# A hybrid attention and state-space layer on one core: k, its row factors and y loaded two tiles ahead, the last filler weights in front of the row factors, a head's loads tied one step earlier

## The chip, the cores and the metric

The kernel runs on 1 core of one Trainium2 chip. The metric is device time in microseconds (us) of one execution. The core's engines are TensorE (PE: matmuls, with weight loads shown apart as PEld), VectorE (DVE), ScalarE (ACT), GpSimd (POOL) and SyncE (SP). SP computes nothing here: nearly every transfer between the core's memory (SBUF) and HBM is issued by it, one after the other in a written order, and an issue that waits holds up every issue behind it. The other engines also work through their instructions in order.

## The reference

One layer over 1024 tokens of 2048 channels, batch 1, everything float32, cut to what the change touches:

```python
h = rms_norm(x, ln_gain)
q, k, v, z_att, u, z_ssm, g_att, g_ssm = split(h @ w_in)      # 2048 x 10240
q, k = rms_norm(q, q_gain), rms_norm(k, k_gain)               # rows of 64
s = q @ k.T / 8                       # 8 heads, two maps each, causal
w = softmax(s[0]) - lam * softmax(s[1])
attn = rms_norm(w @ v, subln_gain) * (1 - lam_init)
y_att = attn * silu(z_att)
y = gelu(s5_scan(u))                  # diagonal state-space branch
y_ssm = y * sigmoid(y @ w_glu + b_glu) * silu(z_ssm)
merged = sigmoid(g_att) * (y_att @ w_proj_att) + sigmoid(g_ssm) * (y_ssm @ w_proj_ssm)
out = x + merged @ w_out
```

## The kernel before

Every operand of a large matmul is split into a high and a low part (`split`: ACT copies the value to a rounded type, DVE subtracts to get the rest), and a product is three matmuls: high by high, high by low, low by high. All tiles are 128 partitions by 512 columns of float32, 256 KB each. Results that are needed later go to HBM (`d_k`, `d_ks`, `d_yg`, `d_zs`, `d_o` and so on) and come back.

The stages in order of time:

1. **Input projection.** 40 column pairs of `w_in`, in two halves of the contraction. A pair is seven products of 12 matmuls, 84 matmuls (a scheme with fewer block products than the plain one). In the second pass (`whole`) each pair's four result tiles go through an evacuation by kind: q (4 pairs), k (4), v (4), `za` (4), `zs` (4), `ga` (8), `gs` (8). Per pair DVE has 16 instructions besides: seven `w_lo`, four `value`, one `acc`, four for the result tiles. `evac_k` stores raw k to `d_k` and collects its squares. `evac_gate` for `zs` also multiplies by y, loaded from `d_yg`.
2. **k's normalisation, between the pairs of `ga` and `gs`.** `norms_k` takes 16 tiles of k: load the tile `ks` from `d_k`, load its row factors `rb` from `d_rk` (two transfers, each a row repeated over 64 partitions), multiply on DVE (L1028), split (ACT writes `sh_`, DVE writes `sl_`), store both parts. `ks` and `rb` have one buffer each, `sh_` two and `sl_` one. Tile n+1's `ks` load therefore waits for tile n's last reader, the subtraction that writes `sl_`. The y tiles of `zs` use the same single buffer as `ks`; the small tile `ny` of `qk_norms` uses that of `rb`.
3. **The sigmoid-gated linear unit** (`pg`, L1162), which writes `d_ys`.
4. **Attention, 8 heads of 8 steps** in an order of PE written out by hand. Between its matmuls stand those of a filler, the projection `w_ps` (`ps_tile`, L288), whose weights come through `branch_weights`: 64 blocks, one loaded ahead. Head h's 14 loads (q, k high, k low, v high, v low: `qs`, `kh`, `kl`, `vh`, `vl`) are tied to the exponentials of head h-1 (`marks`), two to each.
5. **The tail.** Row factors of the attention output (`fr`, `fs`) go to HBM (`d_f`) and come back repeated over 128 partitions (`pf`). `pa_inputs` loads the output (`pr`), multiplies (L1375) and splits it. Three filler tiles, kept back (`TAIL`), run on PE meanwhile: six weight blocks. Then come the projection `w_pa` (L271) and the product with `w_out` (L1409), for each half of the tokens.

Outside the hand-ordered part of PE, a scheduler decides each engine's order from the written order, the buffers and its own estimate of durations; the hardware then follows that order strictly.

Of the kernel before, what the change touches and what calls it, by code (L numbers as in the profile page):

```python
# [10 lines left out]
F32 = mybir.dt.float32  # L11
# [8 lines left out]
P = 128  # L20
# [3 lines left out]
KT = DM // P  # L24
NT = S // P
# [9 lines left out]
TAIL = 3  # L35
# [32 lines left out]
def hybrid_block(ctx: ExitStack, tc: tile.TileContext, x_t, x_n, w_t, w_v, w_glu, w_pa, w_ps,  # L68
                 w_out, small, lams, ssm_bc, out):
    nc = tc.nc  # L70
    V, A, Q, T, D = nc.vector, nc.scalar, nc.gpsimd, nc.tensor, nc.sync

    def after(ins, other):

        tc.add_manual_dep(ins.ins, other.ins.name,
                          mybir.DependencyInfo(mybir.DependencyClass.Sync, mybir.DependencyReason.DATA),
                          reason="order of loads")
# [11 lines left out]
    def split(hi, lo, src, eng=None):  # L89
        A.activation(hi, src, AF.Copy)  # L90
        (eng or V).tensor_tensor(lo, src, hi.bitcast(F32), ALU.subtract)  # L91

    def load_w(src, n, eng=None, pool=None):

        pool, bufs = (wps[0], 2) if pool is None else (pool, 4)
        raw = pool.tile([P, n, WT // n], F32, name="w_raw", tag="w_raw", bufs=bufs)
        D.dma_start(raw, src)
        hi = pool.tile([P, n, WT // n], F32R, name="w_hi", tag="w_hi")
        lo = pool.tile([P, n, WT // n], F32R, name="w_lo", tag="w_lo")
        split(hi, lo, raw, eng)  # L100
        return hi, lo
# [123 lines left out]
    d_yg = dram.tile([8, P, S], F32, name="d_yg")  # L225
    d_ys = [dram.tile([8, P, S], F32, name=f"d_ys{i}") for i in range(2)]
    d_ps = dram.tile([KT, P, S], F32, name="d_ps")
    d_o = dram.tile([H, P, S], F32, name="d_o")
# [67 lines left out]
    def branch_weights():  # L296

        def blocks():
            for n in range(2 * KT):
                for b in range(2):  # L300
                    yield load_w(w_ps[n % KT, :, 4 * b:4 * b + 4], 4, Q if n < 2 * KT - TAIL else V)
        it = blocks()
        queue = [next(it)]

        def take():
            queue.append(next(it, None))
            return queue.pop(0)
        return take

    def finished(src, t):  # L310

# [14 lines left out]
    with ExitStack() as pa_ctx:  # L326
# [315 lines left out]
        rows = [normed(k) for k in range(8, 16)]  # L642
# [290 lines left out]
        for i, (_, n) in enumerate(order):  # L933
            part(n, a, 1)
            while units < min(NPAIR, (i + 1) * NPAIR / PACE):
                ssm_step(units)
                units += 1
                if units == NPAIR:
# [3 lines left out]
                    rows = [row(xp) for _ in range(8)]  # L942
# [9 lines left out]
        ev_ctx = ExitStack()  # L952
        stg = ev_ctx.enter_context(tc.tile_pool(name="stg", bufs=2, side="right"))
        more.append(stg)
        qp = ev_ctx.enter_context(tc.tile_pool(name="qp", bufs=5, side="right"))


        rq = const.tile([P, 16, NT], F32, name="rq")
# [4 lines left out]
        def qk_norms():  # L963

            for t in range(2):
                v = stg.tile([32, 512], F32, name="nv", tag="sq")
                y = stg.tile([32, 512], F32, name="ny", tag="rb", bufs=1)
                V.tensor_scalar(v, nps[t][0:32], 1.0 / 64, EPS, ALU.mult, ALU.add)
                newton_rsqrt(stg, y, v, "nr")
                D.dma_start(d_rk[:, t * 512:(t + 1) * 512], y[16:32])  # L970
                yield
                tp = sps.tile([P, 4, 32], F32, name="rqp", tag="tr", bufs=2)
                for j in range(4):
                    T.transpose(tp[:, j], y[:, j * P:(j + 1) * P], ident[0:32, 0:32])
                V.tensor_copy(rq[:, :, 4 * t:4 * t + 4].rearrange("p a t -> p t a"), tp[:, :, 0:16])
            V.tensor_scalar(nrq, rq, -1.0, None, ALU.mult)
# [35 lines left out]
        def norms_k():  # L1012

            def load(n):
                h, t = divmod(n, 2)
                st = stg.tile([P, 512], F32, name="ks", tag="ks", bufs=1)
                D.dma_start(st, d_k[h, :, t * 512:(t + 1) * 512])
                rb = stg.tile([P, 512], F32, name="rb", tag="rb", bufs=1)
                for c in range(2):
                    D.dma_start(rb[64 * c:64 * c + 64],  # L1020
                                d_rk[2 * h + c:2 * h + c + 1, t * 512:(t + 1) * 512].to_broadcast([64, 512]))
                return st, rb
            ahead = load(0)
            for n in range(16):
                yield
                h, t = divmod(n, 2)
                st, rb = ahead
                V.tensor_tensor(st, st, rb, ALU.mult)  # L1028
                hi, lo = split_tiles()
                split(hi, lo, st)  # L1030
                store2([d[h, :, t * 512:(t + 1) * 512] for d in d_ks], hi, lo)
                if n < 15:
                    ahead = load(n + 1)

        def evac_v(h, t, st):
            tp = sps.tile([P, 512], F32, name="vt", tag="tr", bufs=2)
# [3 lines left out]
            split(hi, lo, tp)  # L1040
            store2([d[h, :, t * 512:(t + 1) * 512] for d in d_vs], hi, lo)

        def evac_gate(dst, silu, src=None):
            def f(i, t, st):
                if silu:
                    sg = stg.tile([P, 512], F32, name="sg", tag="sq")
                    A.activation(sg, st, AF.Sigmoid)
                    if src is not None:
                        y = stg.tile([P, 512], F32, name="y", tag="ks", bufs=1)
                        D.dma_start(y, src[i, :, t * 512:(t + 1) * 512])  # L1050
                        V.tensor_tensor(st, st, y, ALU.mult)
                    Q.tensor_tensor(st, st, sg, ALU.mult)
                else:
                    A.activation(st, st, AF.Sigmoid)
                D.dma_start(dst[i, :, t * 512:(t + 1) * 512], st)
            return f
# [4 lines left out]
        for i, (kind, n) in enumerate(order):  # L1061
            f, m = evacs[kind], n - first[kind]
            whole(n, a, 0, lambda c, t, st, f=f, m=m: f(2 * m + c, t, st), qp, None, w)
            w = None
            if n == 9:
                steps = qk_norms()
            if n in (9, 11, 13):
                next(steps, None)
            if i == 20:
                ks = norms_k()  # L1070
            if i >= 20:
                next(ks, None)
# [18 lines left out]
        ahead = gate_weights(0)  # L1091
# [7 lines left out]
        marks = {}  # L1099

        def head_steps(h):

            n = itertools.count()

            def load(dst, src):
                ins = D.dma_start(dst.bitcast(F32), src)
                i = next(n)
                if h:
                    after(ins, marks[(h - 1) * NT + 1 + i // 2])
            qs, kh, kl, vs = tiles = [], [], [], []  # L1110
            for c in range(2):
                rows = slice(64 * c, 64 * c + 64)
                q_, k1, k2 = (kq.tile([P, S], F32R, name=n, tag=f"{n}{c}") for n in ("qs", "kh", "kl"))
                for e in range(2):
                    for x, d_ in ((q_, d_qs[e]), (k1, d_ks[0]), (k2, d_ks[1])):
                        load(x[64 * e:64 * e + 64], d_[h, rows])
                        yield tiles
                qs.append(q_)
                kh.append(k1)
                kl.append(k2)  # L1120
            for n_, d_ in zip(("vh", "vl"), d_vs):
                vs.append(kq.tile([P, NT, P], F32R, name=n_, tag=n_))
                load(vs[-1], d_[h].rearrange("p (t c) -> p t c", c=P))
                yield tiles
# [22 lines left out]
        load = yg_inputs(1, lambda: gl.tile([P, 512], F32, name="ya", tag="ya", bufs=4))  # L1147
        for k in range(8):
            load(k, ya[1][0][k], ya[1][1][k])
        for ct in range(8):  # L1150
            ws, ahead = ahead, gate_weights(ct + 1) if ct < 7 else None
            for t in range(2):
                tk = slice(t * 512, (t + 1) * 512)
                if 2 * ct + t > 1:
                    next(head0, None)
                r = gl.tile([P, 512], F32, name="r", tag="r", bufs=3)
# [13 lines left out]
            if ct == 6:  # L1170
                ps_weights = branch_weights()
# [8 lines left out]
    with ExitStack() as at:  # L1180
# [81 lines left out]
        late = []  # L1262
# [51 lines left out]
        with tc.manual_schedule(engines={T.engine}):  # L1314
            for h in range(H):
# [3 lines left out]
                for n, tt in enumerate(ORDER):  # L1319
                    i = h * NT + n  # L1320
# [39 lines left out]
    prp = ctx.enter_context(tc.tile_pool(name="prp", bufs=2))  # L1360
# [3 lines left out]
    wp2 = ctx.enter_context(tc.tile_pool(name="wp2", bufs=4))  # L1364

    def pa_inputs(t, pool):
        tk = slice(t * 512, (t + 1) * 512)
        late = []

        def ld(k, hi, lo):  # L1370
            r = prp.tile([P, 512], F32, name="pr", tag="pr", bufs=4)
            D.dma_start(r, d_o[k, :, tk])
            f = prp.tile([P, 512], F32, name="pf", tag="pf", bufs=3)
            D.dma_start(f, d_f[k:k + 1, tk].to_broadcast([P, 512]))
            V.tensor_tensor(r, r, f, ALU.mult)  # L1375
            late.append((hi, lo, r))
            if k:
                split(*late[k - 1])
            if k == 7:
                split(*late[k])  # L1380
        return act_half(pool, ld)

    halves = [pa_inputs(0, mg)]
    for ct in range(KT - TAIL, KT):
        run(ps_tile(1, ct, psa[0], bank(ac2), ps_weights))
# [107 lines left out]
```

## Time and profile before

| what | value |
|---|---|
| runs | median 2738.85 us of 3 (2737.41 to 2740.82) |
| profiled execution | 2741.47 us, its span 2739.7 us |
| mean granted TensorE clock | 0.994 |
| PE busy | 2675.3 us (98%), 12402 matmuls |
| DVE, ACT, POOL busy | 1845.8 us (67%), 1195.8 us (44%), 715.7 us (26%) |
| transfers on SP's queue | 259424 packets, 481.20 MB, 54.7% of the 16 DMA engines' time |

The span runs from the first to the last instruction; the rest of the execution's time lies around it. A busy PE is not PE at its full rate: in the last matmul stage 768 matmuls take 174.08 us in the chain of waits, 0.227 us each, and that is what a full rate is here. "Granted clock" is the share of its full clock that TensorE had in a stretch. The view of waits says which engine's instruction waited for whom: total, number of times, longest.

### The profile page before, as it was taken

How to read it: one execution, taken by the hardware profiler on the slowest of the kernel's cores; microseconds unless marked ns; L12 is line 12 of the kernel's file. 1: busy time of each engine (PE TensorE's matmuls, PEld its weight loads, DVE VectorE, ACT ScalarE, POOL GpSimd, SP SyncE). 2: the span in 40 equal slices, each digit the busy share in tenths (PEclk: the TensorE clock that was granted, in tenths of full speed). 3: DMA queues.
4: the chain of work that ended last, by engine and by line, in shares of the span. 5: the costliest groups of instructions: out<-in, count | busy, mean ns of one | idle time of the engine just before them, and what ended most of it. 6: DMA issues, size and time to landing. Idle time of an engine off the chain costs nothing. (4 is left out here: it accounts for less than half of the span.)

```text
span 2739.7 us, 37819 instructions
## 1 busy us (share of the span) xinstructions
PE 2675.3 (98%) x12402; PEld 2197.7 (80%) x12402; DVE 1845.8 (67%) x3512; ACT 1195.8 (44%) x2343; POOL 715.7 (26%) x1085
## 2 busy tenths in 40 slices
PE   9999999999999999999998999999999989999999
PEld 8888788887788877888876788777878878888887
DVE  4998877778777798779876666456767574325432
ACT  6433555554455456434334444445555443223221
POOL 0001855566755012224431222012222200000000
PEclk9999999999999999999999999999999999999999
DMA  9653333333233456465577655976787485545453
GB/s 353 209 194 121 100 116 120 118 116 118 97 116 118 174 174 197 145 202 173 192 236 241 219 163 169 287 230 201 208 246 200 147 289 183 154 131 186 146 159 113
DMA packets 259621, 483.61 MB, mean 177 GB/s; under 512 B 33656, under 2 KB 44224, under 8 KB 259424
## 3 DMA queue, kind: packets, MB, share of 16 engines
q1 hardware_dynamic: 259424, 481.20, 54.7%
q8 instruction: 97, 1.59, 0.2%
q14 instruction: 100, 0.82, 0.1%
HBM read 341.52 MB, written 139.56 MB: 176 GB/s over the span
## 5 line engine op out<-in xcount | busy, mean ns | idle before, releaser
L497 PE MATMUL acc<-ah,w_hi 128*128 128x512 f32 x2128 | 839.7, 395 | 24.5 <-ACT u L532 19.0
L497 PE MATMUL acc<-ah,w_lo 128*128 128x512 f32 x2128 | 839.9, 395 | 0.0
L497 PE MATMUL acc<-al,w_hi 128*128 128x512 f32 x2128 | 838.6, 394 | 0.0
L90 ACT ACTIVATE w_hi<-w_raw 128x512 fp32r<-128x512 f32 x516 | 323.9, 629 | 527.7 <-PE o L1409 240.1
L91 DVE TENSOR_TENSOR w_lo<-w_raw,w_hi 128x512 fp32r<-128x512 f32 x458 | 324.1, 708 | 288.1 <-ACT w_hi L90 279.5
L497 PEld LDWEIGHTS acc<-ah,w_hi 128*128 128x128 f32 x2128 | 401.6, 189 | 116.0 <-ACT u L532 23.5
L497 PEld LDWEIGHTS acc<-ah,w_lo 128*128 128x128 f32 x2128 | 401.3, 189 | 86.8 <-issue 5.4
L497 PEld LDWEIGHTS acc<-al,w_hi 128*128 128x128 f32 x2128 | 401.6, 189 | 83.0 <-issue 2.0
L90 ACT ACTIVATE w_hi<-value 128x512 fp32r<-128x512 f32 x304 | 191.3, 630 | 321.5 <-DVE value L346 192.1
L91 DVE TENSOR_TENSOR w_lo<-value,w_hi 128x512 fp32r<-128x512 f32 x304 | 229.4, 755 | 60.3 <-ACT w_hi L90 52.6
L1409 PE MATMUL o<-w_hi,ml 128*128 128x512 f32 x512 | 199.3, 389 | 0.0
L1409 PE MATMUL o<-w_lo,mh 128*128 128x512 f32 x512 | 199.3, 389 | 0.0
L1409 PE MATMUL o<-w_hi,mh 128*128 128x512 f32 x512 | 195.4, 389 | 0.0
L346 DVE TENSOR_TENSOR value<-w_raw 128x512 f32<-128x512 f32 x152 | 160.5, 1056 | 2.8
L584 POOL TENSOR_TENSOR p<-p,q 128x512 f32<-128x512 f32 x36 | 61.9, 1719 | 379.2 <-DVE acc L525 269.1
L91 POOL TENSOR_TENSOR w_lo<-w_raw,w_hi 128x512 fp32r<-128x512 f32 x58 | 79.1, 1366 | 298.9 <-ACT w_hi L90 235.0
L590 POOL TENSOR_TENSOR u<-u,q 128x512 f32<-128x512 f32 x72 | 101.3, 1407 | 167.7 <-ACT u L519 88.0
L1212 DVE TENSOR_SCALAR_CACHE_REDUCE pe<-s,nrq 128x128 f32<-128x128 f32 (+7 forms) x128 | 100.2, 813 | 56.3 <-PE s L1208 55.5
L288 PE MATMUL pc<-ah,w_hi 128*128 128x512 f32 x256 | 105.9, 414 | 12.3 <-ACT w_hi L90 5.9
L1409 PEld LDWEIGHTS o<-w_hi,mh 128*128 128x128 f32 x512 | 96.1, 188 | 20.0
L1409 PEld LDWEIGHTS o<-w_lo,mh 128*128 128x128 f32 x512 | 96.1, 188 | 19.9
L1409 PEld LDWEIGHTS o<-w_hi,ml 128*128 128x128 f32 x512 | 96.1, 188 | 19.9
(503 smaller groups left out, 4543.6 us busy)
## 6 DMA issues: line engine op xcount, KB each, us to landing
w_raw<-in_w_t_dram SPq DMA_DIRECT2D x288, 256.0 KB
q<-d_p SPq DMA_DIRECT2D x160, 256.0 KB
w_raw<-in_w_out_dram SPq DMA_DIRECT2D x128, 256.0 KB
d_p<-u SPq DMA_DIRECT2D x72, 256.0 KB
w_raw<-in_w_ps_dram SPq DMA_DIRECT2D x64, 256.0 KB
w_raw<-in_w_pa_dram SPq DMA_DIRECT2D x64, 256.0 KB
d_p<-ps SPq DMA_DIRECT2D x52, 256.0 KB
d_p<-p SPq DMA_DIRECT2D x36, 256.0 KB
```

Source lines behind the costliest of these rows:

```text
L90: A.activation(hi, src, AF.Copy)
L91: (eng or V).tensor_tensor(lo, src, hi.bitcast(F32), ALU.subtract)
L288: T.matmul(ps, lhsT=w[:, k % 4], rhs=b[k], start=(k == 0 and n == 0), stop=(k == 7 and n == 2))
L346: V.tensor_tensor(t, x, y, ALU.add)
L497: T.matmul(ps, lhsT=x[:, c], rhs=y[i][j], start=(start and j == 0 and n == 0), stop=(j == 3 and n == 2), skip_group_check=True)
L584: e.tensor_tensor(u, u, other(1), ALU.add)
L590: e.tensor_tensor(u, u, other(i), ALU.subtract)
L1212: V.tensor_scalar(pc[c][:, 0:w], sc[c][:, 0:w], nrq[:, 2 * h + c, tt:tt + 1], None, ALU.mult, ALU.min, accum_out=mx[:, c:c + 1])
L1409: T.matmul(ps[i], lhsT=a[k][:, tt], rhs=w[:, 0], start=(k == 0 and n == 0), stop=(k == KT - 1 and n == 2))
```

## The change

- **k two tiles ahead.** `ks` and `rb` take two buffers each (those of `nh` and `nl`, which the norms no longer need by then). Two tiles are loaded before the first step and tile n+2's loads are asked for at the end of step n. `sl_` keeps its one buffer.
- **y two tiles ahead.** The same `nh` buffers hold y; a generator issues the loads in the order of use, two before the first `zs` pair. `ny` gets a buffer of its own and the q pool (`qp`) a sixth.
- **Last filler weights.** The last three of the 64 blocks come from the pool `wp2`, which is idle until then. `ps_weights(5)` asks for the five blocks not yet loaded before `pa_inputs` is written. `pr` tiles are loaded six ahead, in place of four buffers taken one by one.
- **Heads' loads.** Each is tied to one step earlier: steps 0 to 6 of the head before, instead of 1 to 7.

No instruction is added or removed on any engine (PE 11693 rows, DVE 3386, ACT 2137, POOL 1090, SP 1882 in both programs); PE's order of work differs only in a few rows, among them the transposition of `fr` and the place where filler and `w_pa` meet.

```diff
                 for b in range(2):
-                    yield load_w(w_ps[n % KT, :, 4 * b:4 * b + 4], 4, Q if n < 2 * KT - TAIL else V)
+                    last = 2 * n + b >= 4 * KT - 3
+                    yield load_w(w_ps[n % KT, :, 4 * b:4 * b + 4], 4, Q if n < 2 * KT - TAIL else V,
+                                 last_pool[0] if last else None)
...
-        def take():
-            queue.append(next(it, None))
-            return queue.pop(0)
+        def take(n=1):
+            while len(queue) <= n:
+                queue.append(next(it, None))
+            return queue.pop(0) if n == 1 else None
...
-        qp = ev_ctx.enter_context(tc.tile_pool(name="qp", bufs=5, side="right"))
+        qp = ev_ctx.enter_context(tc.tile_pool(name="qp", bufs=6, side="right"))
...
-                y = stg.tile([32, 512], F32, name="ny", tag="rb", bufs=1)
+                y = stg.tile([32, 512], F32, name="ny", tag="ny", bufs=1)
...
-                st = stg.tile([P, 512], F32, name="ks", tag="ks", bufs=1)
+                st = stg.tile([P, 512], F32, name="ks", tag="nh")
...
-                rb = stg.tile([P, 512], F32, name="rb", tag="rb", bufs=1)
+                rb = stg.tile([P, 512], F32, name="rb", tag="nl")
...
-            ahead = load(0)
+            ahead = [load(0), load(1)]
...
-                st, rb = ahead
+                st, rb = ahead.pop(0)
...
-                if n < 15:
-                    ahead = load(n + 1)
+                if n < 14:
+                    ahead.append(load(n + 2))
...
+        def y_steps():
+            for m in range(4):
+                for c, t in ((0, 0), (1, 1), (0, 1), (1, 0)):
+                    y = stg.tile([P, 512], F32, name="y", tag="nh")
+                    D.dma_start(y, d_yg[2 * m + c, :, t * 512:(t + 1) * 512])
+                    y_loads[2 * m + c, t] = lambda y=y: y
+                    yield
...
-                        y = stg.tile([P, 512], F32, name="y", tag="ks", bufs=1)
-                        D.dma_start(y, src[i, :, t * 512:(t + 1) * 512])
+                        y = y_loads[i, t]()
                         V.tensor_tensor(st, st, y, ALU.mult)
+                        next(ahead, None)
...
-                    after(ins, marks[(h - 1) * NT + 1 + i // 2])
+                    after(ins, marks[(h - 1) * NT + i // 2])
...
+        def ahead(k):
+            rows.append(prp.tile([P, 512], F32, name="pr", tag="pr", bufs=6))
+            D.dma_start(rows[k], d_o[k, :, tk])
+        for k in range(6):
+            ahead(k)
...
+                if k < 3:
+                    ahead(k + 5)
...
+    last_pool.append(wp2)
+    ps_weights(5)
     halves = [pa_inputs(0, mg)]
```

Three places show what the scheduler makes of it. The first is DVE while k is normalised (`ks<-ks,rb` is the multiplication, `sl_` the subtraction after it; `w_lo`, `value`, `acc`, `p`, `q`, `u` belong to the pairs). Before:

```order
L1028 TENSOR_TENSOR ks<-ks,rb 128x512
L91 TENSOR_TENSOR w_lo<-w_raw,w_hi 128x512
L91 TENSOR_TENSOR sl__16114<-ks,sh__16113 128x512
L585 TENSOR_TENSOR p_15156<-acc,p_15156 128x512
L91 TENSOR_TENSOR w_lo<-value,w_hi 128x512
L346 TENSOR_TENSOR value<-value,w_raw 128x512
L1028 TENSOR_TENSOR ks<-ks,rb 128x512
L591 TENSOR_TENSOR u_15171<-acc,u_15171 128x512
L91 TENSOR_TENSOR w_lo<-value,w_hi 128x512
L91 TENSOR_TENSOR w_lo<-w_raw,w_hi 128x512
L91 TENSOR_TENSOR sl__16286<-ks,sh__16285 128x512
```

After:

```order
L91 TENSOR_TENSOR sl__16119<-ks,sh__16118 128x512
L585 TENSOR_TENSOR q<-acc,q 128x512
L1033 TENSOR_TENSOR ks<-ks,rb 128x512
L91 TENSOR_TENSOR w_lo<-w_raw,w_hi 128x512
L530 TENSOR_TENSOR acc<-acc,p_15161 128x512
L91 TENSOR_TENSOR w_lo<-value,w_hi 128x512
L351 TENSOR_TENSOR value<-w_raw 128x512
L91 TENSOR_TENSOR sl__16291<-ks,sh__16290 128x512
L1033 TENSOR_TENSOR ks<-ks,rb 128x512
```

Multiplications of k now stand closer together: from the first to the last of the 16 there are 105 other DVE instructions before and 87 after, 15 of them the tiles' own `sl_` in both, and one `sl_` can follow the one before after only four to nine others.

The second is DVE where the tail begins (`fs` the row factors, `pr` the multiplication by them, `w_lo` a weight's low part). Before:

```order
L91 TENSOR_TENSOR w_lo<-w_raw,w_hi 128x512 x2
L1356 COPY fs<-fp 64x128
L292 TENSOR_TENSOR z<-z,pc 128x512
L91 TENSOR_TENSOR w_lo<-w_raw,w_hi 128x512
L1375 TENSOR_TENSOR pr<-pr,pf 128x512
L91 TENSOR_TENSOR w_lo<-w_raw,w_hi 128x512
L91 TENSOR_TENSOR al<-pr,ah 128x512
```

After:

```order
L91 TENSOR_TENSOR w_lo<-w_raw,w_hi 128x512
L1376 COPY fs<-fp 64x128
L91 TENSOR_TENSOR w_lo<-w_raw,w_hi 128x512
L292 TENSOR_TENSOR z<-z,pc 128x512
L91 TENSOR_TENSOR w_lo<-w_raw,w_hi 128x512 x4
L1400 TENSOR_TENSOR pr<-pr,pf 128x512 x2
L292 TENSOR_TENSOR z<-z,pc 128x512
```

Four weight blocks are now split between `z` and the first `pr`, where one was.

The third is SP around the last loads of a head (`kl`, `vh`, `vl`; `w_raw` is a filler weight, `z` a filler tile's gate). Before:

```order
L1106 DMA kl<-d_k_76 64x1024
L97 DMA w_raw<-in_w_ps_dram 128x512
L1106 DMA vh<-d_v_77 128x1024
L1106 DMA vl<-d_v_78 128x1024
L293 DMA d_ps<-z 128x512
```

After:

```order
L1126 DMA kl<-d_k_76 64x1024
L282 DMA z<-d_gs 128x512
L1126 DMA vh<-d_v_77 128x1024
L1126 DMA vl<-d_v_78 128x1024
L97 DMA w_raw<-in_w_ps_dram 128x512
```

The head's last loads now stand ahead of the filler weight block that they followed.

More of the change, by code (lines that the diff above doesn't have):

```diff
@@ L300, in blocks @@
                 for b in range(2):
-                    yield load_w(w_ps[n % KT, :, 4 * b:4 * b + 4], 4, Q if n < 2 * KT - TAIL else V)
+                    last = 2 * n + b >= 4 * KT - 3
+                    yield load_w(w_ps[n % KT, :, 4 * b:4 * b + 4], 4, Q if n < 2 * KT - TAIL else V,
+                                 last_pool[0] if last else None)
         it = blocks()
         queue = [next(it)]
-        def take():
-            queue.append(next(it, None))
-            return queue.pop(0)
+        def take(n=1):
+            while len(queue) <= n:
+                queue.append(next(it, None))
+            return queue.pop(0) if n == 1 else None
         return take
+    last_pool = []
     def finished(src, t):
@@ L1041, in evac_v @@
             store2([d[h, :, t * 512:(t + 1) * 512] for d in d_vs], hi, lo)
+        y_loads = {}
+        def y_steps():
[5 more added lines that the diff above has]
+                    yield
+        ahead = y_steps()
         def evac_gate(dst, silu, src=None):
@@ L1068, in hybrid_block @@
                 next(steps, None)
+            if i == 15:
+                next(ahead)
+                next(ahead)
             if i == 20:
@@ L1367, in pa_inputs @@
         tk = slice(t * 512, (t + 1) * 512)
-        late = []
+        late, rows = [], []
+        def ahead(k):
[3 more added lines that the diff above has]
+            ahead(k)
         def ld(k, hi, lo):
-            r = prp.tile([P, 512], F32, name="pr", tag="pr", bufs=4)
-            D.dma_start(r, d_o[k, :, tk])
+            r = rows[k]
             f = prp.tile([P, 512], F32, name="pf", tag="pf", bufs=3)
```

## Prediction

> **What bounds the kernel now.** I read the page first, then the view of waits for PE, then the stretches where PE waits.
>
> ```profile
> span 2739.7 us, 37819 instructions
> PE 2675.3 (98%) x12402; PEld 2197.7 (80%) x12402; DVE 1845.8 (67%) x3512; ACT 1195.8 (44%) x2343; POOL 715.7 (26%) x1085
> ...
> PE acc L497 <- ACT u L532: 19.0, 10, 4.6
> PE pc L288 <- ACT w_hi L90: 5.9, 1, 5.9
> PE pc L288 <- DVE z L292: 5.3, 3, 3.1
> PE s L1205 <- DMA kl<-d_k: 4.0, 6, 0.9
> PE s L1205 <- DMA kh<-d_k: 3.2, 3, 1.8
> ```
>
> PE is the bound: it idles 64.4 us of the span, and the change adds no work to it. What can be won are waits like these. The largest lies where k is normalised, 1395 to 1560 us:
>
> ```profile
> L497 PE MATMUL acc<-ah,w_hi 128*128 128x512 f32 x198 | 81.2, 410 | 20.8 <-ACT u L532 15.8 <-DVE u L591 2.6 <-DVE p L585 1.9
> L1028 DVE TENSOR_TENSOR ks<-ks,rb x16: 692/693/1677, 1403.0 to 1543.6; 128x512 f32<-128x512 f32 x16
> DVE ks L1028 <- DMA rb<-d_rk: 15.7, 3, 5.7
> DVE ks L1028 <- DMA ks<-d_k: 13.4, 8, 3.4
> DVE ks L1028 <- DMA d_ga<-q: 7.7, 3, 3.2
> DVE ks L1028 <- DMA q<-d_p: 5.7, 1, 5.7
> DVE ks L1028 <- DMA d_ga<-p: 4.6, 1, 4.6
> 2300.83 174.08 PE o L1409 x768
> ```
>
> PE's three groups there have 198 matmuls each, 594; at full rate (last row, 174.08 / 768 = 0.227 us) they need 134.7 of the 165 us, so **30.3 us are lost**: 20.8 idle, the rest a slower TensorE clock. PE names ACT and DVE, but these are the second link: DVE, which works in order, stands 47.1 us before `ks` (the five rows added), behind transfers. One turn, from DVE's and SP's timelines:
>
> ```profile
> 1457.33 0.69 DVE L1028 TENSOR_TENSOR ks<-ks,rb 128x512 f32<-128x512 f32 x1 [0.68 <-DMA ks<-d_k]
> 1458.72 0.69 DVE L91 TENSOR_TENSOR sl__16114<-ks,sh__16113 128x512 fp32r<-128x512 f32 x1
> 1460.24 0.41 SPq L994 DMA_DIRECT2D d_k<-sl__16114  x1
> 1460.71 0.43 SPq L1017 DMA_DIRECT2D ks<-d_k  x1
> 1466.50 0.69 DVE L1028 TENSOR_TENSOR ks<-ks,rb 128x512 f32<-128x512 f32 x1 [4.65 <-DMA d_ga<-p]
> ```
>
> The one `ks` buffer is read until 1459.41, the next load is issued at 1460.71, and the next multiplication starts at 1466.50: a turn of 9.2 us, while DVE had other work for half of it only.
>
> **The change, part by part.** Every engine executes as many instructions as before, so each part is a wait removed and what then is late next.
>
> *k two tiles ahead.* Two loads in flight halve that turn. The scheduler has used it: 15 turns now take 87 other DVE instructions instead of 105, of which 72 and 90 belong to column pairs (16 to a pair of 84 matmuls, 19.0 us at full rate). PE thus asks for 72 / 16 x 19.0 = 85.7 us where it asked for 107.1 and got 140.6 (first to last start above). What limits the 15 turns now? Durations for three candidates:
>
> ```profile
> 1400.00:1546.00 146.00, 127.46 (x528) 101.27 (x527) 94.34 (x130) 57.44 (x102) 27.56 (x19) 0.96 0.73 243
> 1560.00:1655.00 95.00, 95.00 (x421) 78.70 (x420) 61.17 (x81) 42.05 (x70) 21.26 (x15) 1.00 0.52 166
> 2020.00:2060.00 40.00, 33.38 (x180) 28.23 (x180) 20.89 (x56) 17.18 (x41) 7.78 (x7) 0.96 0.96 278
> ...
> 1529.92 5.14 DMA rb<-d_rk
> 1538.58 5.02 DMA ks<-d_k
> 1546.47 2.88 DMA d_k<-sl__17594
> 2020.21 6.93 DMA vl<-d_v
> 2032.63 8.63 DMA w_raw<-in_w_ps_dram
> ```
>
> (In the first three rows the columns after the span are busy time and count of PE, weight loads, DVE, ACT and POOL, then granted clock, DMA share, GB/s.) First, DVE's own work: 94.34 / 130 = 0.73 us each, (87 + 16) x 0.73 = 75 us, below 85.7. Second, the new wait: `sl_` keeps one buffer, so a tile's subtraction waits until the store of the tile before has landed. A turn of that is 0.69 (subtraction) + 0.83 (1459.41 to the store's issue at 1460.24) + the landing. Landing is unknown at the new pace: 2.88 us, the one row of such a store, at the low end, 8.63 us in the fullest stretch at the other. I take 5.0, as the two loads beside that store took, since the DMA engines get fuller: 15 x 6.5 = 98 us. Third, the DMA engines: the k work was 0.73 x 146 less the pairs' 0.52 x 120 (528 matmuls at full rate), 44 us of all engines, 15/16 of it with 0.52 x 85.7 makes 86 us; at 98 us a share of 0.88, between the two rows, so 5.0 fits. PE then loses 98 - 85.7 = 12 us of the 30.3: **gain 18**. Ends: at 2.88 a turn is 4.4, 66 us, no loss and a gain of 30; at 8.63 it is 10.2, 152 us, a loss of 67. Behind the waiting `sl_` in DVE's queue stand `w_lo` and the results of pairs, for which PE waits; SP's store and the next `ks` load come after it too.
>
> A page bears on that landing. The Trainium skill's "DMA: Bandwidth & Descriptors", in the section on the anatomy of one DMA, fits 2.0 us plus bytes / 436 GB/s (there for GpSimd's path), 2.6 us for 256 KB as an estimate; by it the sum would have no k loss, 12 us better. The rows of 5.02 and 5.14 us in this stretch are twice that, so the trace decides for the slower value.
>
> *y two tiles ahead.*
>
> ```profile
> DVE q L1051 <- DMA y<-d_yg: 1.8, 2, 1.0
> ```
>
> DVE waits for y twice, and ACT's copy `u` and PE after it; outside the k stretch `u` costs PE 19.0 - 15.8 = 3.2 us in four waits. **Gain 2** (0 to 3). The sixth `q` buffer, `ny`'s own buffer and the earlier `rb` loads lie beside a full PE; SP may wait for the store to `d_rk` before the first `rb`, with weights five and q six buffers deep behind it: 0 (loss up to 3).
>
> *Heads' loads a step earlier.* PE waited 4.0 + 3.2 = 7.2 us for `kl` and `kh` of seven heads, longest 1.8. A step is an eighth of a head:
>
> ```profile
> 1907.63 4.83 PE op L1242 x24
> 1949.15 4.58 PE op L1242 x24
> ```
>
> 41.5 / 8 = 5.2 us, more than the longest of these waits, so they end; next late is the softmax, for which PE already waits a little. **Gain 6** (2 to 8.5, the upper end with the lost rate after a wait).
>
> *Beside it, where 16 loads of `d_ys` come in one burst* (2020 to 2056), a filler weight now stands ahead of the last three and the gate `z` ahead of the last seven, in place of behind all.
>
> ```profile
> 2043.34 7.29 DMA w_raw<-in_w_ps_dram
> 2052.57 3.89 PE pc L288 x9
> ```
>
> PE waited 3.1 us (`z`, longest) before that last row and then ran 9 matmuls at 0.43 us. **Gain 2** (-3 to 5).
>
> *Last filler weights.*
>
> ```profile
> 2198.33 0.77 PE L288 MATMUL pc<-ah,w_hi 128*128 128x512 f32 x1 [5.87 <-ACT w_hi L90]
> 2197.59 0.63 ACT L90 ACTIVATE w_hi<-w_raw 128x512 fp32r<-128x512 f32 x1
> 2194.30 0.69 DVE L1375 TENSOR_TENSOR pr<-pr,pf 128x512 f32<-128x512 f32 x1 [5.72 <-DMA pf<-d_f]
> ...
> 2198.33 7.81 PE pc L288 x24
> ...
> 2209.53 5.44 PE pc L288 x24
> 2214.97 6.73 PE pc L271 x30
> ```
>
> ACT and DVE stood before `pr`, which waited for the row factors, with filler weights queued behind. PE lost 5.87 us, then 7.81 - 5.44 = 2.4 at the slow clock. With the weights in front that goes. But then `pr` is late for the first `w_pa` tile: its last nine matmuls ended at 2214.97 + 9 x 0.227 = 2217.0, and its last `al` was written by 2213.4:
>
> ```profile
> 2212.75 0.69 DVE L91 TENSOR_TENSOR al<-pr,ah 128x512 fp32r<-128x512 f32 x1 [0.70 <-ACT ah L90]
> ```
>
> Two `w_lo` (1.4 us) leave that row of work for DVE's idle 5.72 us, so `al` is there at about 2212.0 and the tile ends near 2212.7. **Gain 4** (0 to 8).
>
> **Sum:** 2 + 18 + 6 + 2 + 4 = 32 us. The profiled execution took 2741.5 us (2739.7 of span and 1.8 around it), 2.6 above the median of the runs, 2738.85; it becomes 2709.5, and the median of runs about **2707**.
>
> **Rivals.**
>
> 1. *The k loads and stores land in time.* With a landing near 2.88 us there is no loss in the k stretch: 12 us more, 2695, and lower if the tail gives its 8. For it: that row, and a share of 0.73 that leaves room. Against it: at 85.7 us the DMA engines would need 86, a share of 1.0. This is what that page's fit of 2.6 us would give.
> 2. *The k stretch keeps its loss.* Before, DVE's order also ran ahead of the transfers, and the turn was 9.2 us where the order had work for 7. If turns come out at 7.7 us, a landing of 6.2, 15 take 116 us, PE loses 30 as before, the gain is 14: 2725.
> 3. *Slower: the store of `sl_` in a full DMA ring.* From a landing of 7.2 us a turn is 8.7, the 15 take 131 us, PE loses 45 and the other 14 us are eaten; at the 8.63 us of the burst row the loss is 67 and the time 2762. For it: both rows over 6.9 us. Against it: they belong to a stretch at a share of 0.96, and a longer k stretch empties the ring, 86 / 131 being 0.66.
> 4. *The change doesn't do what it says*: PE's removed waits come back elsewhere, as waits for DVE in attention and in the tail: gain within 5, 2736.
>
> **How the numbers follow.** Forecast 0.50 (2698 to 2717), rival 1 0.20 (2690 to 2698), rival 2 0.20 (2717 to 2730), rival 3 0.05, rival 4 0.05. A change of 0.2%, 5.5 us, is about what a measurement of this kernel tells from none; the first three lie beyond it. Faster 0.91, same 0.05, slower 0.04. Leaving out one in ten on each side, the range takes half of rival 1's cases and half of rival 2's: 2693 to 2726.
>
> **What would show it.** In the k stretch: DVE's waits at `ks` gone, waits of `sl_` for the transfer `d_k<-sl_` in their place, the 16 multiplications within 92 to 105 us, a DMA share near 0.85, PE losing about 12 us. No wait of DVE for y. No wait of PE for `kh` or `kl`. In the tail no wait for `w_hi` of 5.9 us, but one of PE's `w_pa` tiles for `al` or `ah`. The prediction is wrong if 16 multiplications take over 115 us, or under 90.

## The result, and the profile after

The changed kernel takes 2699.75 us (median of runs, 2698.58 to 2704.01) beside 2738.85 for the kernel before: a ratio of 0.9855, 95% interval 0.984 to 0.9869, some 39 us. A fourth run of the kernel before, at 4762.93 us, is left out of this. Timed once more it was 2701.67, ratio 0.9861 (0.9847 to 0.9876). The forecast was 2707, range 2693 to 2726.

The page (the profile's summary), and PE's waits after the change:

```profile
span 2697.7 us, 37815 instructions
PE 2664.3 (99%) x12402; PEld 2195.0 (81%) x12402; DVE 1843.1 (68%) x3512; ACT 1197.9 (44%) x2343; POOL 714.6 (26%) x1085
...
PE pc L288 <- ACT ah L90: 6.2, 1, 6.2
PE pc L288 <- DVE z L292: 4.1, 3, 1.9
PE pc L271 <- DVE z L1426: 2.9, 1, 2.9
...
PE acc L502 <- ACT u L537: 2.1, 3, 1.0
```

The 19.0 us of waits for `u` are 2.1, and `kl` and `kh` are gone from the list. But a wait of 6 us stands before a filler tile as it did before (5.9), and one of 2.9 us in the projection `w_pa` is new.

Three events cut the span into stretches: the start of the last projection matmul `acc`, of the last attention matmul `osm`, and of the first output matmul `o`. Of each row only the first and the last start are read here, the kernel before first:

```profile
L497 PE MATMUL acc<-ah,w_hi x2128: 387/389/794, 103.1 to 1728.9; 128*128 128x512 f32 x194
L1259 PE MATMUL osm<-ones,osq x128: 165/251/272, 1872.3 to 2172.4; 128*128 128x2 f32 x128
L1409 PE MATMUL o<-w_hi,mh x512: 388/389/390, 2300.7 to 2735.2; 128*128 128x512 f32 x171
```

and after:

```profile
L502 PE MATMUL acc<-ah,w_hi x2128: 387/389/504, 102.4 to 1695.5; 128*128 128x512 f32 x194
L1279 PE MATMUL osm<-ones,osq x128: 165/251/272, 1833.9 to 2126.5; 128*128 128x2 f32 x128
L1438 PE MATMUL o<-w_hi,mh x512: 389/389/389, 2258.7 to 2693.2; 128*128 128x512 f32 x171
```

| us | to the last `acc` | to the last `osm` | to the first `o` (the tail) |
|---|---|---|---|
| before | 1728.9 | 443.5 | 128.3 |
| after | 1695.5 | 431.0 | 132.2 |
| gain | 33.4 | 12.5 | -3.9 |
| forecast | 20 | 8 | 4 |

From the first `o` on both take 434.5 us. The middle column holds the gated linear unit and attention. So the time came out near the forecast with none of its three parts the right size: that it lies so near is partly luck.

**The k stretch.** DVE's multiplications of k, its waits, the stretch by windows and PE's first group in the 165 us shown of before:

```profile
L1033 DVE TENSOR_TENSOR ks<-ks,rb x16: 676/683/693, 1393.9 to 1484.2; 128x512 f32<-128x512 f32 x16
...
DVE sl__15431 L91 <- DMA d_k<-sl__15259: 3.9, 1, 3.9
DVE sl__17151 L91 <- DMA d_k<-sl__16979: 2.2, 1, 2.2
DVE sl__15947 L91 <- DMA d_k<-sl__15775: 1.9, 1, 1.9
DVE sl__17594 L91 <- DMA d_k<-sl__17495: 1.9, 1, 1.9
DVE ks L1033 <- DMA ks<-d_k: 1.5, 2, 0.8
...
1390.00:1485.00 95.00, 93.35 (x408) 75.82 (x407) 78.71 (x110) 45.89 (x83) 23.55 (x16) 1.00 0.97 323
...
L502 PE MATMUL acc<-ah,w_hi 128*128 128x512 f32 x239 | 93.2, 391 | 1.6 <-ACT u L537 1.0 <-DVE p L590 0.4
```

The 47.1 us of waits at `ks` are 1.7 (1.5 and a last row of 0.2), and in their place DVE waits at `sl_` for the store of the tile before, as forecast. But it does so at seven of the fifteen `sl_` that could wait, 11.6 us in all; at the other eight the store had already landed. The sixteen multiplications span 90.3 us in place of 140.6. PE runs 3 x 239 = 717 matmuls in the 165 us, 162.5 us at full rate: it loses 2.5 us where it lost 30.3.

### The profile page after: what moved, and what is told of

It is laid out like the page before. It is cut to its first block, busy times and chain, and to the rows that moved or that the text cites. A ratio compares the mean times of both kernels' runs of the same rounds, so it can differ in the third digit from the quotient of the medians.

```text
span 2697.7 us, 37815 instructions
## 1 busy us (share of the span) xinstructions
PE 2664.3 (99%) x12402; PEld 2195.0 (81%) x12402; DVE 1843.1 (68%) x3512; ACT 1197.9 (44%) x2343; POOL 714.6 (26%) x1085
## 4 chain that ended last, share of the span: by engine, by line
PE 82%; DMA 8%; DVE 6%; POOL 2%; issue 1%; ACT 1%; SPq 1%; DVEq 0%; ACTq 0%; POOLq 0%
PE acc L502 43%; PE o L1438 13%; PE pc L271 6%; PE pc L288 5%; PE acc L481 3%; PE pg L1182 2%; PE s L1225 2%; PE op L1262 2%; DVE w_lo L91 1%; DMA ya<-d_yg 1%; PE tp L1250 1%; PE gp L858 1%; DMA w_raw<-in_w_ps_dram 1%; DMA w_raw<-in_w_t_dram 1%; DVE value L351 1%
```

## The experiments

The stretches of all kernels below, read from the same three rows of each trace:

| us | to the last `acc` | to the last `osm` | tail |
|---|---|---|---|
| 1 k and y alone | 1697.1 | 438.5 | 128.7 |
| 2 heads alone | 1724.6 | 430.3 | 128.5 |
| 3 tail alone | 1729.8 | 440.8 | 132.7 |
| 4 without the tail's edit | 1696.2 | 429.4 | 129.1 |
| 5 changed kernel, two banks | 1697.2 | 428.3 | 127.0 |
| 6 two banks, `fs` elsewhere | 1698.2 | 430.1 | 129.8 |
| 7 as 4, two `sl_` | 1697.7 | 431.3 | 129.2 |
| 8 as 4, two banks | 1700.5 | 431.1 | 130.4 |
| 9 as 5, `fp` earlier | 1697.3 | 430.7 | 127.7 |
| 10 as 4, `rb` twice only | 1702.1 | 430.1 | 131.4 |
| 11 changed kernel again | 1698.3 | 435.1 | 133.1 |
| 12 as 5, again | 1698.6 | 431.4 | 124.3 |

Row 11 against "after" and row 12 against row 5 show how far a stage moves with nothing changed: up to 4 us (rows 5 and 12 come from two different chips, which may be part of it). So a stage's effect is read from the kernels with an edit against those without it, not from one pair.

**1 to 4: which part brings what.** The first three are the kernel before with one part of the diff each; the fourth is the changed kernel with the tail's part taken back:

```diff
-    last_pool.append(wp2)
-    ps_weights(5)
     halves = [pa_inputs(0, mg)]
...
-                                 last_pool[0] if last else None)
...
-            r = rows[k]
+            r = prp.tile([P, 512], F32, name="pr", tag="pr", bufs=4)
+            D.dma_start(r, d_o[k, :, tk])
```

> The kernel before with the k and y part alone (two buffers of ks and rb, y by the generator, the sixth q buffer); heads' loads and tail as before. Theory A, read from the two traces (the last input-projection matmul starts 33.4 us earlier after the change): these edits bring 33 us whatever the others do, so the profiled span is 2739.7 - 33 = 2707, give or take 2, and from that matmul on every stage is as long as before. Theory B, the terms of the prediction (18 + 2): 20 us, 2720; the other 13 us would then come from an interplay with the other edits. The 16 multiplications of k take 90 us, with waits of sl_ for its store, under both.

> The kernel before with the heads' loads alone tied one step earlier. Theory A (stage times of the two traces: attention is 12 to 14 us shorter after the change, and this edit is the only one inside it): 12 us, span 2727.5 give or take 2; no wait of PE for kh or kl, and the wait of 3.1 us for z in the burst of d_ys loads falls to about 1.9. Theory B (the prediction's terms, 6 + 2, the rest of the shift coming from the tail's edit to the filler weights): 8 us, 2732, with the 3.1 us wait unchanged.

> The kernel before with the last filler weights' part alone (three blocks from the pool wp2, five blocks asked for ahead, output tiles six ahead). Theory A (from the last attention matmul to the first output matmul 128.3 us before and 132.2 after): this edit costs 4 us, span 2744, and PE's wait of about 6 us before a filler tile stays. Theory B (the prediction): a gain of 4, 2736. Theory C: the 4 us are lost only because the tail is reached with more transfers in flight; then this edit alone is worth 0 give or take 1.

> The changed kernel with that tail part undone and all else kept. Theory A: 4 us faster than the changed kernel, span 2693.7, and from the last attention matmul to the first output matmul 128 us as before. Theory B: 4 us slower, 2702. Theory C: the stretch is over 130 us without the edit too, span 2697.7 give or take 1.

Measured, by medians of runs: k and y alone 0.9893 (0.9867 to 0.9919), spans 2703.3; heads alone 0.9961 (0.9949 to 0.9972), span 2722.4; the tail alone 1.0009 (0.9997 to 1.0021), span 2742.3; without the tail's edit 0.9851 (0.9828 to 0.9875), span 2693.7. By the table: the kernels with the k and y part reach the last `acc` at 1695.5 to 1702.1, those without at 1724.6 to 1729.8, about 30 us. The middle stretch takes 428.3 to 435.1 us with the heads' edit and 438.5 to 443.5 without, about 10. The tail takes 132.2 to 133.1 with its edit (after, 3, 11) and 128.3 to 129.2 without (before, 1, 2, 4, 7; only 10 stands apart at 131.4), a loss of some 4. By these stretches theory A is the nearer one in all four, with the heads at 10 rather than 12; the spans of 1 and 2 lie 2 to 3 us beyond its bounds, on the side away from theory B. But the profiled executions of 1, 2 and 4 were the fastest of their runs, 8.3, 4.8 and 6.1 us below the median, so their spans flatter the edits. By medians the gains are 27, 11.5, -3 and 39 us: for experiment 1 that lies midway between the 33 of theory A and the 20 of theory B, and the tail's 4 us are not resolved, since experiments 3 and 4 alone don't exclude 0.

Why the heads' edit brought 10 to 13 us where the waits for `kl` and `kh` were 7.2, attention by windows, before and with the heads' edit alone:

```profile
1817.00:2173.00 356.00, 334.71 (x1852) 287.73 (x1853) 245.52 (x589) 192.44 (x439) 91.74 (x68) 0.99 0.70 203
...
1813.00:2155.00 342.00, 330.09 (x1850) 285.94 (x1850) 246.44 (x587) 192.56 (x439) 92.59 (x68) 1.00 0.74 211
```

Idle time falls from 21.3 to 11.9 us, and PE's busy time for the same matmuls (two of them not recorded) by 4.6, at a granted clock of 1.00 in place of 0.99: that fits the slow matmuls behind each wait, which go with it.

**5: what PE waits for in the tail.** A bank holds one tile of matmul results until another engine has read it. In the trace of the changed kernel, the wait of PE, ACT's rows that end near its end, and DVE's:

```profile
2152.70 0.76 PE L288 MATMUL pc<-ah,w_hi 128*128 128x512 f32 x1 [6.15 <-ACT ah L90]
...
2151.99 0.63 ACT L90 ACTIVATE ah<-pr 128x512 fp32r<-128x512 f32 x1 [0.22 <-DVE pr L1400]
...
2147.80 0.69 DVE L91 TENSOR_TENSOR w_lo<-w_raw,w_hi 128x512 fp32r<-128x512 f32 x1 [3.61 <-ACT w_hi L90]
2149.14 1.37 DVE L91 TENSOR_TENSOR w_lo<-w_raw,w_hi 128x512 fp32r<-128x512 f32 x2 [0.64 <-ACT w_hi L90]
2150.42 0.69 DVE L1400 TENSOR_TENSOR pr<-pr,pf 128x512 f32<-128x512 f32 x1
2151.27 0.69 DVE L1400 TENSOR_TENSOR pr<-pr,pf 128x512 f32<-128x512 f32 x1 [0.16 <-DMA pf<-d_f]
2151.88 0.68 DVE L292 TENSOR_TENSOR z<-z,pc 128x512 f32<-128x512 f32 x1
```

The view names ACT's copy `ah`, which ends at 2152.62. A filler tile has no use for it. DVE's `z`, which empties the one bank of the filler's results (`ac2`, bufs=1), ends at 2152.56, behind the last weights' `w_lo` and two `pr`. The test gives the last three tiles two banks:

```diff
-        run(ps_tile(1, ct, psa[0], bank(ac2), ps_weights))
+        run(ps_tile(1, ct, psa[0], bank(ac3), ps_weights))
```

> The changed kernel with the last three filler tiles in the two PSUM banks of the projection after them, in place of one bank. In the changed kernel PE waits 6.15 us in front of a filler tile; the view of waits names ACT's copy of an output tile (ah), which ends at 2152.62, but the gate's multiplication z of the tile before, which empties the one bank, ends at 2152.56 on DVE, behind four w_lo and two pr. Theory A (PE waits for z): this wait goes, and PE next waits for the parts of the output (al) in the first tile of the projection, last written at about 2168; from the last attention matmul to the first output matmul 129 to 130 us in place of 132.2, span about 2695. Theory B (the wait is for ACT, as the view says, or for the weights): 6 us of wait stay before a filler tile, 132 us, span 2697.7.

PE's waits in the tail with two banks:

```profile
PE pc L271 <- ACT ah L90: 4.5, 3, 2.1
PE pc L288 <- ACT ah L90: 0.6, 1, 0.6
PE pc L271 <- DVE al L91: 0.5, 2, 0.2
```

The 6.15 us before a filler tile are 0.6; what is left stands before the projection, for its inputs. Tail 127.0, span 2691.5, median 2696.66, ratio 0.984 (0.9823 to 0.9856). PE did wait for `z`: theory A, with more gain than it expected. The scheduler also no longer puts 13 matmuls of the projection between the last two filler tiles, but the wait that went lies ahead of that place.

**6 and 9: is the chain of the row factors next?** Experiment 6 also moves `fs` (`fs = const.tile(...)`), so that the last weights' buffers no longer lie where `fs` lay. In the changed kernel these weights were not in front of the row factors at all, by SP's timeline:

```profile
2139.05 0.37 SPq L97 DMA_DIRECT2D w_raw<-in_w_ps_dram  x1
2139.51 0.47 SPq L1377 DMA_DIRECT2D d_f<-fs  x1
2142.12 0.33 SPq L282 DMA_DIRECT2D z<-d_gs  x1
2142.97 1.28 SPq L97 DMA_DIRECT2D w_raw<-in_w_ps_dram  x3
```

Experiment 9 keeps the fifth's two banks and puts `fp` 39 filler matmuls behind the last `osm` instead of 51:

```diff
+            feed(24)
+            feed(14)
+            fr = tiny.tile([P, H, NT], F32, name="fr", tag="fr", bufs=1)
...
+            T.transpose(fp, fr.rearrange("p h t -> p (h t)"), ident)
             for _ in range(KT):
                 feed(24)
```

> The same two banks, and the row factors' tile fs taken from a pool whose memory the last weights do not reuse. Theory A (the first of the last three weight loads waits until the store of fs has landed, since it takes the memory of fs's pool; so these weights were never in front of the row factors): two of the three weight loads are issued before that store, their w_lo end 3 us earlier, the first pr is no longer behind them, and the stretch from the last attention matmul to the first output matmul is 1 to 2 us shorter than with the two banks alone, about 128 us. Theory B (the row factors' own chain, store, load, multiplication, split, is what ends last): no shorter than with the two banks alone, within 0.7 us.

> The changed kernel with the two banks of the fifth experiment, and the row factors' transposition fp placed 39 filler matmuls behind the last attention matmul in PE's written order in place of 51, no work changed. Theory A (what ends last in the tail is now the chain of the row factors: fp, fs, its store to d_f, the loads pf, pr, ah and al): everything in this chain moves up by 2 to 2.5 us and the stretch from the last attention matmul to the first output matmul falls from 127.0 to about 125. Theory B (DVE's and ACT's own work on weights and outputs there is the limit): within 0.7 us of 127.0.

In experiment 6 two of the weight loads do go ahead, at the cost of the store `d_f`, which is now behind them:

```profile
2141.28 0.91 SPq L97 DMA_DIRECT2D w_raw<-in_w_ps_dram  x2
2142.25 0.52 SPq L1377 DMA_DIRECT2D d_f<-fs  x1
2142.82 1.05 SPq L97 DMA_DIRECT2D w_raw<-in_w_ps_dram  x2
```

The first `pr` then starts 21.9 us after the last `osm` in place of 23.9 in experiment 5, as theory A said, but the tail is 129.8 us, not shorter than 127.0; median 2699.2, ratio 0.9848. Experiment 9 has 127.7, median 2698.19, ratio 0.9848, which looks like theory B. But the edit did not do what it was meant to: `fs` is written 2.5 us earlier (9.7 us after the last `osm`, 12.1 in experiment 5), and its store leaves SP only 0.2 us earlier (12.8 after, 13.0 in 5), because a filler weight's load issued at 2139.87 and a store of `z` stand ahead of it in SP's order. So the chain behind that store was not moved up, and whether it is what ends last stays open. Experiment 9's PE waits again 3.2 us for a `z` in the projection. The DMA engines are 0.91 and 0.93 busy there in experiments 5 and 9 (windows 2126 to 2180 and 2127 to 2183), DVE for 37 of 54 and 41 of 56 us; both edits left some waits in the tail and brought new ones.

**8: two banks without the early weights.**

> The kernel of the fourth experiment with the last filler tiles in two banks. There PE waits 6.46 us for w_hi, which ACT writes behind a copy of an output tile. Theory A: without the early weights a second bank is worth nothing, the wait for w_hi stays at 6 to 7 us and the stretch from the last attention matmul to the first output matmul at 129 us, span 2694 give or take 1. Theory B (the single bank is what holds PE in both): the wait falls under 2 us and the stretch to 127 or less.

```profile
PE pc L271 <- DVE z L1412: 2.6, 2, 2.0
PE pc L271 <- ACT ah L90: 1.8, 2, 1.0
PE pc L288 <- DVE fs L1371: 1.3, 1, 1.3
```

Half of each theory: the 6.5 us named `w_hi` is gone (longest 1.3 before a filler tile), so the single bank held PE here too; and the tail, 130.4, is no shorter. In experiment 4 `z` ended at 2152.02 and the `w_hi` that is named at 2152.10, and PE went on at 2152.16. In experiment 8 ACT writes that `w_hi` behind the same two `ah`, at 2158.03, and PE had begun the filler tile at about 2153 without it. Median 2702.4, ratio 0.9857 (0.9842 to 0.9872). With early weights and the second bank together the tail was shorter in 5, 9 and 12 (124.3 to 127.7), though not in 6.

**7 and 10: what limits k now?** Experiment 7 gives `sl_` a second buffer (`tag="sl_", bufs=2`) in the kernel of experiment 4. Experiment 10, from the same kernel, loads `rb` for two tiles only:

```diff
-                rb = stg.tile([P, 512], F32, name="rb", tag="nl")
+                if n < 2:
+                    rbs.append(stg.tile([P, 512], F32, name="rb", tag="nl"))
...
-                return st, rb
+                return st, rbs[n % 2]
```

> The kernel of the fourth experiment (k, y and heads, without the tail's edit) with two buffers of sl_. Theory A (a tile of k now takes 6.0 us because sl_ waits for the store of the one before): DVE's waits of sl_ for that store, 11 us in the fourth experiment, are gone, the 16 multiplications take 84 to 87 us in place of 89.7, PE loses under 1 us there in place of about 2, span 2692 give or take 1. Theory B (the DMA engines, at a share of 0.97 there, are what limits it): the waits move to ks for its loads with about the same sum, the 16 multiplications still take 89 to 91 us, and the span stays at 2693.7.

> The kernel of the fourth experiment in which the row factors rb are loaded for the first two tiles of k only and used again for the other fourteen, so k is scaled by the wrong rows: 28 transfers of 128 KB fewer, 3.7 MB of the 30.7 MB that move in the 95 us of the k stretch. The scheduler then puts 69 other DVE instructions between the first and the last multiplication in place of 87, a pace of 64 us for PE. Theory A (the DMA engines' total is the limit: 44 us of k's own work less 11, and 0.52 of the time for the pairs): the 16 multiplications take 66 to 72 us, a share of 0.95 or more, landings no longer than before, PE losing under 6 us. Theory B (the turn of the one sl_ buffer, 1.5 us and a landing of 4.6, is the limit): 15 turns of 6.1 us, 90 us, and PE loses over 15 us.

With two `sl_` buffers, DVE's multiplications and waits:

```profile
L1028 DVE TENSOR_TENSOR ks<-ks,rb x16: 673/691/1541, 1393.0 to 1480.5; 128x512 f32<-128x512 f32 x16
...
DVE ks L1028 <- DMA rb<-d_rk: 5.8, 4, 2.2
DVE ks L1028 <- DMA ks<-d_k: 5.6, 4, 3.6
```

The waits at `sl_` for a store are gone and 12.5 us of waits for transfers stand at `ks` (the two rows and one of 1.1), where experiment 4 had 11.2 at `sl_` and 1.8 at `ks`; 87.5 us in place of 89.7, span 2697.2, median 2697.8, ratio 0.9839 (0.9825 to 0.9854), which overlaps that of experiment 4. Theory B but for the 2 us: the single `sl_` buffer is where DVE waits, the transfers are why. Without most `rb` loads (one run, 2704.86 us):

```profile
L1030 DVE TENSOR_TENSOR ks<-ks,rb x16: 680/688/693, 1393.6 to 1469.5; 128x512 f32<-128x512 f32 x16
...
1390.00:1485.00 95.00, 88.74 (x380) 71.62 (x379) 75.06 (x108) 44.60 (x80) 23.14 (x16) 0.98 0.84 282
```

75.9 us, between the theories. A turn is 75.9 / 15 = 5.06 us, less the 1.52 of subtraction and issue at most 3.5 on average for the landing, where the changed kernel has at most 90.3 / 15 - 1.52 = 4.5. With fewer bytes the stores landed sooner, at a share of 0.84. DVE waited for them at eight `sl_`, 10.1 us, and for loads at `ks`, 5.3 us, so neither the one buffer nor the loads alone set the pace. And PE lost more, not less: 380 matmuls in 95 us are 86.1 at full rate, 8.9 lost, where the scheduler's order now asked for 64 us.

**11 and 12: the same kernels again.**

> The changed kernel once more, beside the experiment with the earlier transposition. Theory A (stage times add): its span is 5 to 8 us longer than that experiment's, the whole of it between the last attention matmul and the first output matmul (132.2 against 125). Theory B: within 2 us, the stages' spread from run to run covering it.

> The kernel of the fifth experiment once more, with more rounds. The changed kernel's second profile stood 7.8 us behind its first, in stages that no experiment touched, so a span alone does not carry 5 us. Theory A (the second bank takes 5 us out of the tail): 127.0 us, give or take 0.7, from the last attention matmul to the first output matmul again, and a median of runs of 2695 to 2698, 3 to 5 us under the changed kernel's 2699.75 and 2701.67. Theory B (the fifth experiment was a favourable run): 129 us or more in that stretch, a median within 2 us of the changed kernel's.

The changed kernel: tail 133.1, span 2705.5, 10.8 us behind experiment 9, of which 5.4 in the tail; the rest lies in stages that the edits do not touch. It was the slowest of its runs; the medians, 2701.67 and 2698.19, differ by 3.5, between the two theories. Two banks: tail 124.3, span 2693.3, median 2696.09 (2692.77 to 2698.63), ratio 0.9839 (0.9825 to 0.9852) to the kernel before. Theory A, with a tail shorter still than its 127.0 by more than it allowed. No version that was run has a lower median: 2696.66 and 2696.09 lie 3 to 6 us under the changed kernel's two, though the intervals of the ratios overlap (0.9825 to 0.9852 against 0.9847 to 0.9876), and experiment 7, without the tail's edit, has the same ratio of 0.9839.

## Why the prediction was right, and where it was not

*The mechanism of k* was right: waits at `ks` gone, the store of `sl_` next. The term of 18 us was mis-sized: PE's loss fell from 30.3 to 2.5, a gain of 28. The term let every turn wait for a landing of 5.0, and only seven of fifteen did. Of the 9.5 us between the forecast loss of 12 and 2.5, the turn gives 7.7 (15 turns took 90.3 us, not 98), and 2 are left: a stretch of 90.3 against an order of 85.7 should cost PE 4.6, it cost 2.5. The landings in the chain of waits after the change:

```profile
1403.95 5.53 DMA d_k<-sl__15259
...
1428.78 5.50 DMA d_k<-sl__15947
...
1440.48 4.65 DMA d_k<-sl__16291
...
1452.48 3.75 DMA d_k<-sl__16635
```

On average 4.9, and over all turns 4.5 at most: the 5.0 taken was near for the stores that DVE waited for. The fit of the Trainium skill's "DMA: Bandwidth & Descriptors" (anatomy of one DMA), 2.6 us as an estimate, was not met by any of these rows, though the time came out on its side of the sum. Rival 1 described the loss; its cause, a landing near 2.88, did not happen. The objection to it, that the DMA engines would have to be full, described what came: their share was 0.97, not 0.88, and they kept up. One count was off without touching the sum: between the first and the last multiplication the trace of the kernel before has 109 other DVE instructions, not 105, so its order asked for some 112 us rather than 107.1.

*y*: DVE's waits for y are gone, as forecast; no run separates its gain from that of k.

*Heads' loads and the burst*: 8 forecast, 10 by the table. The waits for `kl` and `kh` ended as forecast, and the longest for `z` in the burst fell from 3.1 to 1.9. The slow matmuls behind each wait, 4.6 us in attention, were left out of the term of 6 and named only for its upper end.

*Last filler weights*: +4 forecast, -4 measured. The step that failed is "with the weights in front that goes": it took PE's 5.87 us as a wait for `w_hi`, the name in the view. In the kernel before, `w_hi` ended at 2198.22 and PE went on at 2198.33, but `z` of the filler tile before had ended at 2198.18:

```profile
2197.50 0.68 DVE L292 TENSOR_TENSOR z<-z,pc 128x512 f32<-128x512 f32 x1
```

Experiment 8 shows, without early weights, which of the two PE waited for: with a second bank the wait went. (In experiment 10, whose tail is written as in the kernel before, both end within 0.01 us of each other and the view names `z`, for 8.1 us.) So weights in front could not take this wait away. Before, `z` stood behind a `pr` that waited 5.72 us for its row factors; after, it stood behind four `w_lo` and two `pr`, as the order shown ahead of the prediction already had it, and the prediction did not ask who waits for it. Second, the weights were in front in DVE's and ACT's order alone: their loads waited for the store of the row factors (2142.97 after 2139.51 above; in experiment 6, with `fs` elsewhere, two of them went first). Third, a new wait of 2.9 us for a `z` in the projection, and after it the slow matmuls, in the chain of waits before and after:

```profile
2229.83 71.00 PE pc L271 x312
...
2184.99 73.84 PE pc L271 x312
```

2.9 + 2.8 us in place of 0.5 + 1.1 is the loss of 4: the granted clock is 0.50 from 2184.99 to 2191 in the changed kernel, and 1.00 behind the wait of 1.1 before. That this `z` came late because the second half's `pr` now stand ahead of it is read from DVE's order, where two `pr`, three `al` and a `w_lo` fill the 3.6 us before it; no run isolated it.

*The sum* of 32 us came near the measured 39 with errors that partly cancel: by the table 10 too few for k and y, 2 too few for the heads, 8 too many for the tail. The mechanisms forecast for k and the heads stood; that of the tail fell, so the near total owes part to luck.

*Of the signs named beforehand*, the multiplications within 92 to 105 us came out at 90.3, at the edge of what was named as wrong; the share near 0.85 was 0.97; no wait for `w_hi` of 5.9 us is there, but one as long under another name; and the projection `w_pa` waits for a `z`, not for `al` or `ah`.

## What to carry to other kernels

When the order of an engine is fixed beforehand, compare the time that it took with the time that the order asks for: here PE's loss was that difference to within some 3 us. A second buffer for the loads cut it from 30 us to 2.5, a further buffer only moved the wait, and fewer bytes with a faster order lost more in the one run made. Before putting work in front in a queue, look for the small instruction that stands behind it and frees a buffer for the bound engine, here a 0.7 us multiplication that empties a bank. And where two instructions end within 0.2 us of a wait's end, the view names one of them: ask which the waiting work uses, and take that one away to be sure. Last, before a test is read, see in its trace that the edit moved what it was meant to move.

## What the runs showed of the hardware

A busy share does not tell how long a transfer takes. Weight loads of 256 KB took 7.29 and 8.63 us in the burst before (share 0.96, 278 GB/s), stores of 256 KB 3.75 to 5.53 us and a weight load 5.67 us in the k stretch after (share 0.97, 323 GB/s); rival 3 had taken the one for the other. A wait of PE costs more than its idle time when it is long enough: behind the wait of 2.9 us in the tail the granted clock was 0.50 for 6 us, behind the one of 5.9 us in the kernel before 0.50 for the first 2.7 us, and behind one of 1.1 us 1.00. And the same program's stages differ from run to run by more than expected: 431.0 and 435.1 us for the middle stretch of the changed kernel, 127.0 and 124.3 for the tail with two banks.
